# First mixer of a two-layer trunk: nineteen block transfers a group on another queue, and a third place between dependent steps of the triangular solve

## The chip, the cores and the metric

The kernel runs on one core of a Trainium2 chip. The core has a matrix engine (TensorE, PE in the profile, its weight loads PEld), a vector engine (VectorE, DVE), an activation engine (ScalarE, ACT), a general engine (GpSimd, POOL) and a synchronising engine (SyncE, SP). Each engine works through its own instructions in order. Transfers between HBM and on-chip memory are issued by SyncE or by GpSimd, each on a queue of its own. The metric is the device time of one execution in microseconds, lower is better.

## The reference

A decoder trunk of two layers works on one sequence of 256 positions with 2048 features, all in float32. Layer 0 mixes with gated DeltaNet, layer 1 with sparse attention; behind each mixer stand a residual layer norm, a gated convolutional feed-forward part and a small gated update. The change lies in the mixer of layer 0, whose core is this (cut):

```python
kb = k * beta[..., None]
vb = v * beta[..., None]
diff = gc[..., :, None] - gc[..., None, :]
decay = jnp.where(tri, jnp.exp(jnp.where(tri, diff, 0.0)), 0.0)
lmat = jnp.where(strict, jnp.einsum('bhncd,bhnsd->bhncs', kb, k) * decay, 0.0)
amat = lmat + jnp.eye(C, dtype=jnp.float32)
rhs = jnp.concatenate([vb, kb * jnp.exp(gc)[..., None]], axis=-1)
sol = lax.linalg.triangular_solve(amat, rhs, left_side=True, lower=True, unit_diagonal=True)
qk = jnp.where(tri, jnp.einsum('bhncd,bhnsd->bhncs', q, k) * decay, 0.0)
...
def step(S, inp):
    v_new = u_n - jnp.einsum('bhck,bhkv->bhcv', w_n, S)
    o_n = jnp.einsum('bhck,bhkv->bhcv', qd_n, S) + jnp.einsum('bhcs,bhsv->bhcv', qk_n, v_new)
    S = S * gl_n[..., None, None] + jnp.einsum('bhck,bhcv->bhkv', kd_n, v_new)
```

Here q, k and v are projections of the input with a short causal convolution, beta and the decays gc come from two small gates, and each of 32 value heads has a unit lower triangular system to solve. The output of each head is normed and gated with a projection z, and a last projection joins the heads.

## The kernel before

**Tiling.** Every large product streams its float32 weights from HBM in pieces of 512 KB (`raw`, four buffers). ScalarE copies each piece into the form that TensorE multiplies (`hi`, line 127), VectorE takes the rest (`lo`, line 128), and TensorE multiplies both; `hi` and `lo` have three buffers each. SyncE's queue carries these pieces, and a piece can be asked for when the `lo` of the piece four before it is written.

**Groups.** The first mixer treats the 32 value heads in eight groups of four. A group's sequence is cut into two halves of 128 positions (index `a`), and each half into four blocks of 32 (index `b`). The order of the weight products is: `values(g)`, then `keys(g + 1)` with the queries, then `zgate(g + 1)`, then the next group. Behind `values(7)` and in place of further keys the output projection is begun (`ahead`).

**Places.** The small work of a group is written as generators that yield. The weight products call `next(self.inter)` after every few matmuls; each call is a place, and the generator runs on to its next yield there. `behind` ties an instruction behind the weight matmul issued last, as order alone, without a semaphore; `late` does the same for all groups but the first, whose front work is emitted at once inside `values(0)`. A planner then orders each engine's instructions by its own estimate of when each is ready, by the order of emission and by raised priorities (the splits of weights, the copies and hops of the solve). An instruction tied to a place can come later than it, not earlier. `pause(n)` leaves n places empty, and `flush` runs what is left of a generator at once.

- `front(g + 1)` runs in the 27 places of `zgate(g + 1)`: `fetch` (the gates' rows, `qd`), `decays` and `sums`, `blocks` (the matrix `L` and its diagonal blocks to `lt` in HBM), `causal` (the masked decays `dm`, in tile `qd`; line 530 clips, line 532 takes the exponential; then the gram `gt`, whose blocks go to `lo` in HBM), and for all groups but the first `pieces` (`ld` read back from `lt`).
- `substitute` inverts the 32 x 32 diagonal blocks on GpSimd out of `ld`, one row after another (lines 685 and 687), and sends them to `tt` in HBM.
- `inverses` loads them into `pm`, and the off-diagonal blocks from `lo` into `LB`. It is called behind `keys(g + 1)`, once the places of the solve before are used up.
- `solve` runs in the places of the next `values` and `keys`, 24 each (42 in all for group 6, where part of the output projection takes the keys' place): per block a product with the inverse (`y_ps`, line 773), ScalarE's copy of it (`ys`, line 776), and for the next block a product with the earlier solutions (`l_ps`, line 766) and VectorE's step to the new right side (`ts`, line 769), called a hop here. Three hops stand in each half.
- `outputs` follows in the same places: two sets of products (`o_ps`), their squares, an inverse root, VectorE's gating (line 806) into `ot`. The transposes of `ot` (line 812) are handed on to the next `zgate` or `ahead`.

In `finish`, the solve and the outputs of one group take 38 yields before the change; group 0 has four more empty places ahead. The mixes of the next group run beside them from the ninth place.

Weights and the transfers of `qd`, `rd`, `lt`, `lo`, `ld`, `rr` and `LB` share SyncE's queue; `tt`, `pm` and the constants are on GpSimd's, which also computes `substitute` in the same order of instructions.

Of the kernel before, what the change touches and what calls it, by code (L numbers as in the profile page):

```python
# [12 lines left out]
AF = mybir.ActivationFunctionType  # L13
# [46 lines left out]
def bcast(ap, n, axis):  # L60

    dims = [list(x) for x in ap.ap]
    dims.insert(axis, [0, n])
    return bass.AP(tensor=ap.tensor, offset=ap.offset, ap=dims)


class Trunk:
# [393 lines left out]
    def gdn_groups(self, pool, gk, cw, ng, oT, load, gates, ahead):  # L461
# [4 lines left out]
        nc, t = self.nc, self.t  # L466
# [3 lines left out]
        LB = pool.tile([P, 2, 6, P], F32, tag="LB", name="LB")  # L470
# [6 lines left out]
        pause = lambda n: itertools.repeat(None, n)  # L477
# [19 lines left out]
        def late(s, ins):  # L497
            return self.behind(ins) if s["g"] else ins
# [19 lines left out]
        def causal(s):  # L518

            g, dm = s["g"], s["qd"]  # L520
            do = s["qo"] = pool.tile([P, 4, P], F32, tag="qo", name="qo", bufs=2)
            for h in h4:
                late(s, nc.scalar.activation(do[:, h], dm[:, 1, h], AF.Exp, bias=self.gout[:, 4 * g + h:4 * g + h + 1]))
            yield
            n21 = s["n21"] = pool.tile([P, 4, P], F32, tag="n21", name="n21", bufs=2)
            nc.vector.tensor_tensor(five(n21), bcast(s["gram"][0][:, :, P:S], 2, 2), five(do), op=ALU.mult)
            for a in range(2):
                for h in h4:
                    gc = self.gc[:, a, 4 * g + h:4 * g + h + 1]
                    late(s, nc.vector.scalar_tensor_tensor(dm[:, a, h], dm[:, a, h], gc, self.qmin,  # L530
                                                           op0=ALU.subtract, op1=ALU.min))
                nc.scalar.activation(dm[:, a], dm[:, a], AF.Exp)
                yield
            gt = s["gt"] = pool.tile([P, 2, 4, P], F32, tag="ld" if g else "L", name="gt")
            for a, ps in enumerate(s["gram"]):
                nc.vector.tensor_tensor(five(gt[:, a]), bcast(ps[:, :, 0:P], 2, 2), five(dm[:, a]), op=ALU.mult)
            yield
            sq = s["sq"] = pool.tile([P, 2, S], F32, tag="y0", name="sq")
            nc.scalar.activation(sq, s["q"], AF.Square)
            xm = s["xm"] = pool.tile([P, 4, 16], F32, tag="xm", name="xm")  # L540
            nc.vector.tensor_tensor(xm, bcast(s["x8"].rearrange("p q e -> p (q e)"), 4, 1), bcast(self.blk, 16, 2),
                                    op=ALU.mult)
            yield from pause(2)
            lo = s["lo"] = self.dr.tile([32, 2, 4, 6, 32], F32, tag="lb", name="lo")
            for c in range(3):
                late(s, nc.sync.dma_start(
                    out=lo.rearrange("k a h n j -> k (a h) (n j)")[:, :, 32 * pair(c, c + 1):][:, :, :96 - 32 * c],
                    in_=gt[32 * c:32 * c + 32, :, :, 32 * c + 32:].rearrange("k a h i -> k (a h) i")))
                yield
            if g:  # L550
                yield
                pieces(s)
# [69 lines left out]
        def blocks(s):  # L622

            g, c, L = (s[x] for x in ("g", "c", "L"))
            for a, ps in enumerate(s["gram"]):
                for h in h4:
                    nc.vector.scalar_tensor_tensor(L[:, h, a], ps[:, h // 2, 0:P], c[:, a, h // 2, h % 2:h % 2 + 1],
                                                   L[:, h, a], op0=ALU.mult, op1=ALU.mult)
                yield
            yield  # L630
            lt = s["lt"] = self.dr.tile([8, 4, 32, 32], F32, tag="lt", name="lt")
            for b in range(4):
                late(s, nc.sync.dma_start(
                    out=lt[:, b].rearrange("q i j -> i q j"),
                    in_=L[32 * b:32 * b + 32, :, :, 32 * b:32 * b + 32].rearrange("p h a j -> p (h a) j")))
            yield

        def pieces(s):

            ld = s["ld"] = pool.tile([P, 32, 32], F32, tag="ld", name="ld")  # L640
            for e in h4:
                late(s, nc.sync.dma_start(out=ld[32 * e:32 * e + 32], in_=bass.AP(
                    tensor=s["lt"].tensor, offset=s["lt"].offset, ap=[[1024, 32], [1, 1024]])))

        def mixes(s):
# [46 lines left out]
        def inverses(s):  # L692

            for h in h4:
                nc.gpsimd.dma_start(out=pm[32 * h:32 * h + 32, :, :, 32 * h:32 * h + 32].rearrange("p a b j -> p (a b) j"),
                                    in_=s["tt"][2 * h:2 * h + 2].rearrange("a b c e j -> (c e) (a b) j"))
            for h in h4:
                for a in range(2):
                    self.behind(nc.sync.dma_start(out=LB[32 * h:32 * h + 32, a, :, 32 * h:32 * h + 32],
                                                  in_=s["lo"][:, a, h]))  # L700

        def values(s):
            g = s["g"]
# [41 lines left out]
        def solve(s):  # L745
            u = s["u"] = pool.tile([P, 2, 4, P], F32, tag="u", name="u")
            bank = lambda name: self.sp.tile([P, P], F32, tag="bk", name=name)
            for a in range(2):
                if a:
                    ps = self.sp.tile([P, 4, 4, 32], F32, tag="bk", name="x_ps")  # L750
                    for h in h4:
                        self.behind(nc.tensor.matmul(ps[:, :, h], u[:, 0, h],
                                                     s["n21"][:, h].rearrange("p (b i) -> p b i", b=4),
                                                     start=True, stop=True))
                    with self.tc.high_priority():
                        nc.vector.scalar_tensor_tensor(s["v1"], ps, -2.0, s["v1"], op0=ALU.mult, op1=ALU.add)
                    yield from pause(2)
                    s["turn"](1)
                    yield from pause(2)
                y = pool.tile([P, 4, P], F32, tag="y", name="ys", bufs=2)  # L760
                for b in range(4):
                    r = s["vs"][:, b]
                    if b:
                        ps = bank("l_ps")
                        for c in range(b):
                            self.behind(nc.tensor.matmul(ps, LB[:, a, pair(c, b)], y[:, c], start=not c, stop=c == b - 1))
                        r = pool.tile([P, P], F32, tag="ts", name="ts")
                        with self.tc.high_priority():
                            nc.vector.scalar_tensor_tensor(r, ps, s["s8"][:, b, 1, a:a + 1], s["vs"][:, b],
                                                           op0=ALU.mult, op1=ALU.add)  # L770
                        yield from pause(2)
                    ps = bank("y_ps")
                    self.behind(nc.tensor.matmul(ps, pm[:, a, b], r, start=True, stop=True))
                    with self.tc.high_priority():
                        if b < 3:
                            nc.scalar.activation(y[:, b], ps, AF.Copy)
                        for h in h4:
                            nc.scalar.activation(u[32 * b:32 * b + 32, a, h], ps[32 * h:32 * h + 32], AF.Copy)
                    yield from pause(2)
                yield  # L780

        def outputs(s):
# [41 lines left out]
        def finish(s, n):  # L824

            steps = [itertools.chain(pause(0 if s["g"] else 4), solve(s), outputs(s))]
            if n is not None:
                steps.append(itertools.chain(pause(8), mixes(n)))
            while steps:
                yield  # L830
                steps = [x for x in steps if next(x, steps) is not steps]

        def front(s):
            return itertools.chain(fetch(s), decays(s), sums(s), blocks(s), causal(s))
# [5 lines left out]
        rest, s = [], keys(0)  # L840
        for g in range(8):
# [18 lines left out]
            if g < 7:  # L860
                substitute(n)
                self.inter = finish(s, n)
                s = n
# [441 lines left out]
```

## Time and profile before

| | us |
|---|---|
| median of 3 runs (2774.4, 2787.5, 2786.63) | 2786.63 |
| the profiled execution | 2776.45 |
| its span | 2773.4 |
| TensorE busy in the span | 2739.2 |
| VectorE, ScalarE, GpSimd busy | 1860.1, 1487.1, 354.3 |

The profiled execution takes 3 us more than its span, which runs from its first to its last instruction. The first mixer's groups fill about the first 765 us; each group takes some 85.

A row of order of time reads: start in us from the span's start, length in us, engine, line, operation, what it writes and from what, shapes, how many were merged into the row; in square brackets the idle time of the engine before it and what ended it. SPq is SyncE's queue. A row of waits reads: who waited, for whom, microseconds in total, number of times, the longest. A row of stretches holds the stretch and its length, then busy time and number of instructions for PE, PEld, DVE, ACT and POOL, the granted TensorE clock as a share of full speed, the DMA engines' share and GB/s. A row of groups ends with total busy us and mean ns of one, then the idle time before them and what ended it.

### The profile page before, as it was taken

What the parts mean: (1) busy time and instruction counts of PE and PEld (TensorE: products, weight loads), DVE (VectorE), ACT (ScalarE), POOL (GpSimd) and SP (SyncE); (2) the same over time, 40 slices, a digit from 0 to 9 for tenths busy, and PEclk for the clock granted to TensorE, in tenths of its full rate; (3) what the DMA queues carried; (4) which work ended last, traced back from release to release, by engine and by line L of the source; (5) the groups of instructions that cost most, each with busy time, mean ns of one, the idle gap of its engine ahead of it and who ended that gap; (6) DMA issues with size and microseconds to landing.
All of it is one profiled execution on the core that took longest, in us unless ns stands there. A gap on an engine that the chain in (4) does not pass through costs nothing. (4 is left out here: it accounts for less than half of the span.)

```text
span 2773.4 us, 40001 instructions
## 1 busy us (share of the span) xinstructions
PE 2739.2 (99%) x14604; PEld 2356.4 (85%) x14604; DVE 1860.1 (67%) x3109; ACT 1487.1 (54%) x2512; POOL 354.3 (13%) x682
## 2 busy tenths in 40 slices
PE   9999999999999999999999999999999999999999
PEld 7888888888888888888888889888888888888887
DVE  7878787877556666666545766775676666655566
ACT  5666666666545555555434544455455555543444
POOL 1554333554000000000000000210000000000000
PEclk9999999999999999999999999999999999999999
DMA  7766767666575666766666567545566666656655
GB/s 224 195 188 169 183 171 181 153 176 175 167 240 162 188 209 203 209 199 203 193 195 206 182 184 232 175 144 165 175 190 197 196 191 194 199 192 191 211 171 193
DMA packets 435140, 525.08 MB, mean 189 GB/s; under 512 B 50976, under 2 KB 324496, under 8 KB 434688
## 3 DMA queue, kind: packets, MB, share of 16 engines
q1 hardware_dynamic: 427952, 504.05, 60.9%
q0 software_dynamic: 6992, 18.49, 2.7%
q8 instruction: 114, 1.87, 0.3%
q14 instruction: 82, 0.67, 0.1%
HBM read 516.62 MB, written 8.97 MB: 190 GB/s over the span
## 5 line engine op out<-in xcount | busy, mean ns | idle before, releaser
L128 DVE TENSOR_TENSOR lo<-raw,hi 128x1024 fp32r<-128x1024 f32 (+1 forms) x920 | 1123.3, 1223 | 600.8 <-ACT hi L127 584.2
L127 ACT ACTIVATE hi<-raw 128x1024 fp32r<-128x1024 f32 (+1 forms) x920 | 966.8, 1053 | 656.4 <-PE mm_ps L202 400.3
L160 PE MATMUL mm_ps<-xT,hi 128*128 128x512 f32 (+1 forms) x4176 | 1036.3, 396 | 6.8 <-DVE xT L242 5.7
L160 PEld LDWEIGHTS mm_ps<-xT,hi 128*128 128x128 f32 (+1 forms) x4176 | 764.8, 189 | 153.8 <-ACT hi L241 5.6
L164 PE MATMUL mm_ps<-xT,lo 128*128 128x256 f32 (+1 forms) x4176 | 557.9, 284 | 0.9 <-DVE lo L128 0.9
L164 PEld LDWEIGHTS mm_ps<-xT,lo 128*128 128x128 f32 (+1 forms) x4176 | 538.3, 191 | 22.1 <-DVE lo L128 1.7
L199 PE MATMUL mm_ps<-hi,xT 128*128 128x512 f32 (+1 forms) x704 | 272.6, 388 | 0.0
L202 PE MATMUL mm_ps<-hi,xT 128*128 128x512 f32 (+1 forms) x704 | 268.8, 383 | 0.0
L237 ACT ACTIVATE fold<-mm_ps 128x256 f32<-128x256 f32 x261 | 98.3, 377 | 266.2 <-PE mm_ps L160 266.0
L199 PE MATMUL mm_ps<-hi,hTA 128*128 128x512 f32 x512 | 199.2, 389 | 0.0
L202 PE MATMUL mm_ps<-hi,hTA 128*128 128x512 f32 x512 | 199.2, 389 | 0.0
L206 PE MATMUL mm_ps<-lo,xT 128*128 128x512 f32 (+1 forms) x704 | 187.8, 383 | 0.0
L256 POOL DMA_DIRECT2D lng<-in_ln_g x16 | 8.8, 551 | 1239.1 <-PE mm_ps L206 661.1
L685 POOL TENSOR_TENSOR xt<-ld,xi 128x60 f32<-128x60 f32 (+24 forms) x248 | 124.4, 501 | 305.3 <-DMA ld<-lt 286.5
L202 PEld LDWEIGHTS mm_ps<-hi,xT 128*128 128x128 f32 x704 | 132.2, 188 | 24.2
L199 PEld LDWEIGHTS mm_ps<-hi,xT 128*128 128x128 f32 x704 | 132.1, 188 | 23.7
L206 PEld LDWEIGHTS mm_ps<-lo,xT 128*128 128x128 f32 x704 | 130.1, 188 | 24.9
L206 PE MATMUL mm_ps<-lo,hTA 128*128 128x512 f32 x512 | 136.8, 389 | 0.0
L687 POOL TENSOR_TENSOR xi<-xi,xt 128x60 f32<-128x60 f32 (+24 forms) x248 | 119.2, 481 | 19.4
L202 PEld LDWEIGHTS mm_ps<-hi,hTA 128*128 128x128 f32 x512 | 96.1, 188 | 20.0
L206 PEld LDWEIGHTS mm_ps<-lo,hTA 128*128 128x128 f32 x512 | 96.1, 188 | 20.0
L199 PEld LDWEIGHTS mm_ps<-hi,hTA 128*128 128x128 f32 x512 | 96.1, 188 | 19.9
(264 smaller groups left out, 2570.4 us busy)
## 6 DMA issues: line engine op xcount, KB each, us to landing
raw<-in_gdn_w_in SPq DMA_DIRECT2D x192, 512.0 KB, 4.8
raw<-in_ffn_w_gate SPq DMA_DIRECT2D x160, 512.0 KB, 4.0
raw<-in_ffn_w_up SPq DMA_DIRECT2D x160, 512.0 KB, 4.1
raw<-in_ffn_w_down SPq DMA_DIRECT2D x160, 512.0 KB, 4.1
raw<-in_dsa_w_in SPq DMA_DIRECT2D x72, 512.0 KB, 3.7
raw<-in_gdn_w_o SPq DMA_DIRECT2D x64, 512.0 KB, 4.0
raw<-in_ple_w_gate SPq DMA_DIRECT2D x64, 512.0 KB, 4.9
raw<-in_dsa_w_o SPq DMA_DIRECT2D x32, 512.0 KB, 3.8
```

Source lines behind the costliest of these rows:

```text
L127: act = nc.scalar.activation(hi, raw, AF.Copy)
L128: ins = nc.vector.tensor_tensor(lo, raw, hi.bitcast(F32), op=ALU.subtract)
L160: ins = nc.tensor.matmul(q[:m, :], hi[:, k, o:o + m], x[:, k0 + k].rearrange("p a b -> p (a b)"), start=k0 + k == 0, stop=last)
L164: ins = nc.tensor.matmul(q[:m, S:], lo[:, k, o:o + m], x[:, k0 + k, 0, :], start=False, stop=last)
L199: ins = nc.tensor.matmul(ps[a][:, :n], xh, hi, start=k == 0, stop=False)
L202: self.before = self.recent = nc.tensor.matmul(ps[a][:, :n], xl, hi, start=False, stop=False)
L206: self.last = self.recent = nc.tensor.matmul(ps[a][:, :n], x(k)[:, 0, a * P:(a + 1) * P], lo, start=False, stop=k == kt - 1)
L237: nc.scalar.activation(t[:m], ps[:, S:], AF.Copy)
L256: ins = self.nc.gpsimd.dma_start(out=r, in_=bass.AP(tensor=src.tensor, offset=src.offset, ap=[[0, P], [1, n]]))
L685: nc.gpsimd.tensor_tensor(tmp[:, :m, :w], bcast(ld[:, i + 1:, i], m, 1), xi[:, :m, i:i + 1].to_broadcast([P, m, w]), op=ALU.mult)
L687: nc.gpsimd.tensor_tensor(xi[:, :m, i + 1:], xi[:, :m, i + 1:], tmp[:, :m, :w], op=ALU.subtract)
```

## The change

Three edits, all in the first mixer:

1. The transfers of `L`'s diagonal blocks to HBM (`lt`, four a group), of the gram's blocks (`lo`, three), the reading back (`ld`, four) and the loading of the off-diagonal blocks (`LB`, eight) are issued by GpSimd in place of SyncE. `LB`'s are no longer tied behind the last weight matmul; the others stay tied as before.
2. Behind each hop of VectorE in the solve, and behind the first product of the first half (`y_ps` of `a` = 0, `b` = 0, which ScalarE copies), three places instead of two.
3. In `causal` each exponential over `dm` is issued one place after the four clips before it and is tied to that place; the gram's products follow one place after the second.

```diff
@@ causal
                     late(s, nc.vector.scalar_tensor_tensor(dm[:, a, h], dm[:, a, h], gc, self.qmin,
                                                            op0=ALU.subtract, op1=ALU.min))
-                nc.scalar.activation(dm[:, a], dm[:, a], AF.Exp)
                 yield
+                late(s, nc.scalar.activation(dm[:, a], dm[:, a], AF.Exp))
+            yield
@@ causal
             for c in range(3):
-                late(s, nc.sync.dma_start(
+                late(s, nc.gpsimd.dma_start(
                     out=lo.rearrange("k a h n j -> k (a h) (n j)")[:, :, 32 * pair(c, c + 1):][:, :, :96 - 32 * c],
@@ blocks
             for b in range(4):
-                late(s, nc.sync.dma_start(
+                late(s, nc.gpsimd.dma_start(
                     out=lt[:, b].rearrange("q i j -> i q j"),
@@ pieces
             for e in h4:
-                late(s, nc.sync.dma_start(out=ld[32 * e:32 * e + 32], in_=bass.AP(
+                late(s, nc.gpsimd.dma_start(out=ld[32 * e:32 * e + 32], in_=bass.AP(
@@ inverses
             for h in h4:
                 for a in range(2):
-                    self.behind(nc.sync.dma_start(out=LB[32 * h:32 * h + 32, a, :, 32 * h:32 * h + 32],
-                                                  in_=s["lo"][:, a, h]))
+                    nc.gpsimd.dma_start(out=LB[32 * h:32 * h + 32, a, :, 32 * h:32 * h + 32], in_=s["lo"][:, a, h])
@@ solve
                             nc.vector.scalar_tensor_tensor(r, ps, s["s8"][:, b, 1, a:a + 1], s["vs"][:, b],
                                                            op0=ALU.mult, op1=ALU.add)
-                        yield from pause(2)
+                        yield from pause(3)
@@ solve
-                    yield from pause(2)
+                    yield from pause(2 if a or b else 3)
```

## The prediction

> **What bounds the kernel now.** I read the page's busy shares first, then the waits of the matmul engine, then order of time around its longest waits.
>
> ```profile
> PE 2739.2 (99%) x14604; PEld 2356.4 (85%) x14604; DVE 1860.1 (67%) x3109; ACT 1487.1 (54%) x2512; POOL 354.3 (13%) x682
> ```
> ```profile
> PE l_ps L766 <- ACT ys L776: 13.0, 6, 2.9
> ...
> PE y_ps L773 <- DMA pm<-tt: 2.9, 1, 2.9
> ...
> PE y_ps L773 <- ACT hi L127: 1.4, 5, 0.3
> ```
>
> TensorE is busy for 2739.2 of 2773.4 us, so no edit to queues and places can bring more than the 34 us in which it is not, and these rows hold 17.3 of them, all in the first mixer's solve. The large one comes once in each of six groups: l_ps, the first product after the first block's solution, waits for ScalarE's first copy. One group in order of time, first TensorE, then ScalarE, then SyncE's queue:
>
> ```profile
> 468.89 1.98 PE L160 MATMUL mm_ps<-xT,hi 128*128 128x512 f32 x8
> 470.71 0.38 PE L773 MATMUL y_ps<-vs,pm 128*128 128x128 f32 x2
> 470.85 2.15 PE L164 MATMUL mm_ps<-xT,lo 128*128 128x256 f32 x16
> 474.86 0.49 PE L766 MATMUL l_ps<-ys,LB 128*128 128x128 f32 x2 [1.85 <-ACT ys L776]
> 475.10 3.51 PE L160 MATMUL mm_ps<-xT,hi 128*128 128x512 f32 x8
> ```
> ```profile
> 468.50 0.63 ACT L532 ACTIVATE qd<-qd 128x512 f32<-128x512 f32 x1 [1.97 <-DVE qd L530]
> 469.03 0.58 ACT L738 ACTIVATE zs<-mm_ps 128x512 f32<-128x512 f32 x1
> 471.63 1.06 ACT L127 ACTIVATE hi<-raw 128x1024 fp32r<-128x1024 f32 x1 [2.01 <-DMA raw<-in_gdn_w_in]
> 472.60 0.61 ACT L532 ACTIVATE qd<-qd 128x512 f32<-128x512 f32 x1
> 473.11 0.58 ACT L738 ACTIVATE zs<-mm_ps 128x512 f32<-128x512 f32 x1
> 473.59 1.04 ACT L127 ACTIVATE hi<-raw 128x1024 fp32r<-128x1024 f32 x1
> 474.54 0.27 ACT L776 ACTIVATE ys<-y_ps 128x128 f32<-128x128 f32 x1
> ```
> ```profile
> 459.43 0.37 SPq L620 DMA_DIRECT2D rd<-rs  x1
> 461.93 3.22 SPq L122 DMA_DIRECT2D raw<-in_gdn_w_in  x2
> 465.25 4.72 SPq L633 DMA_DIRECT2D lt<-L  x4
> 470.06 4.28 SPq L122 DMA_DIRECT2D raw<-in_gdn_w_in  x3
> ```
>
> The copy stands seventh in ScalarE's order. The first exponential holds ScalarE for 1.97 us until VectorE has written its operand; then a split waits 2.01 us for weights; then a second exponential, a tanh and a split stand before the copy. On SyncE's queue the four transfers of L take 4.72 us, and no weight is asked for between 465 and 470.
>
> The eight matmuls from 468.89 to 470.71 are two places of the order, so **a place is 0.91 us**. And a stall is dearer than its idle time: the eight matmuls after it last 3.51 us instead of 1.98. The stretches around the stalls show why; the first and the last of four such rows (the other two are at 471 and at 557):
>
> ```profile
> 386.00:394.00 8.00, 5.07 (x25) 4.29 (x24) 5.89 (x11) 4.12 (x9) 0.00 (x0) 0.79 1.07 311
> ...
> 642.00:650.00 8.00, 6.07 (x26) 4.92 (x25) 4.93 (x7) 5.60 (x14) 0.00 (x0) 0.79 1.00 287
> ```
>
> The column behind POOL is the granted clock: 0.79. By the matmul rows one such drop costs 3.51 - 2.10 = 1.4 us (2.10 as in the row below), four of them 5.6. Two of the six stalls have none; one of them:
>
> ```profile
> 223.97 0.49 PE L766 MATMUL l_ps<-ys,LB 128*128 128x128 f32 x2 [1.78 <-ACT ys L776]
> 224.22 2.10 PE L160 MATMUL mm_ps<-xT,hi 128*128 128x512 f32 x8
> ```
>
> So a gap of 1.78 us kept the clock, and one of 1.85 lost it. [...]
>
> **The change, part by part.**
>
> *A third place behind the first copy.* It puts 0.91 us of weight matmuls between y_ps and l_ps in every group that stalls: 6 x 0.91 = 5.5 us off the 13.0. The copy does not get later by it, as it depends on y_ps alone. It is covered by matmuls that have to run anyway; at the end of the group the cover is thinner, see below.
>
> *Exponentials a place later.* Between the landing of the weights and the copy stands one exponential, 0.51 us from its start to the next. If it goes behind the copy, that is 6 x 0.5 = 3.0; if the planner leaves it, because VectorE and not its place decides when it is ready, nothing. The wait of 1.97 before it is followed by the wait for weights, and so not worth its length by itself. I take half, 1.5.
>
> *Transfers on GpSimd's queue.* SyncE loses 19 issues a group: four of L, three of the gram, four of ld, eight of LB. The next rows show what the eight hold up: they stand before the fetch of the gates' rows, and ScalarE and, behind it, VectorE wait for these.
>
> ```profile
> 276.23 5.04 SPq L699 DMA_DIRECT2D LB<-lo  x8
> 281.37 0.39 SPq L503 DMA_DIRECT2D qd<-grow  x1
> ```
> ```profile
> ACT L L513 <- DMA qd<-grow: 16.4, 6, 3.6
> ```
> ```profile
> L128 DVE TENSOR_TENSOR lo<-raw,hi 128x1024 fp32r<-128x1024 f32 x8 | 9.8, 1219 | 2.5 <-ACT hi L127 2.5
> ```
>
> The fetch can be issued up to 5.0 us earlier, which removes most of 16.4 / 6 = 2.7 us of ScalarE's waiting a group and the 2.5 us that VectorE stands idle in this one. How much reaches the copy is not to be read: the late weights were asked for at 461.93, before L's transfers, so taking those away does not bring them sooner; they land late behind rd, which stays. Only if the whole stretch runs earlier do they. Bounds: nothing, and all that the first two parts leave, 13.0 - 5.5 - 1.5 = 6.0. I take 2.5, somewhat under half, because the weights' own issue is not moved.
>
> [...]
>
> What it costs on GpSimd:
>
> ```profile
> L695 POOL DMA_DIRECT2D pm<-tt x32 | 18.6, 591 | 12.5 <-DMA tt<-xi 12.0
> ```
> ```profile
> L685 POOL TENSOR_TENSOR xt<-ld,xi 128x60 f32<-128x60 f32 (+24 forms) x248 | 124.4, 501 | 305.3 <-DMA ld<-lt 286.5
> ```
> ```profile
> 276.08 2.33 POOL L695 DMA_DIRECT2D pm<-tt  x4
> ```
> ```profile
> 302.70 0.38 PE L773 MATMUL y_ps<-vs,pm 128*128 128x128 f32 x2
> ```
>
> 19 x 0.59 = 11.2 us a group, into 286.5 / 8 = 35.8 us in which GpSimd waits for ld. If LB's eight go ahead of pm, pm's last issue ends 4.7 us later, at 283 instead of 278.4, and the next group's first y_ps needs it at 302.7. In the first group, where pm is late already (the 2.9), the same order falls into GpSimd's wait for tt; there I see between -2.9 and +2 and take 0. Behind pm's wait for tt on GpSimd then stand L's transfers; a substitution that starts some us later still ends within those 20.
>
> *A third place behind each of VectorE's hops.* The five waits of y_ps put down to a split, 1.4 us, are each at most 0.3, under a place. That they are for ts is my reading: the split named is not an operand of y_ps. All of it: -1.4.
>
> *What seven places more push back.* A solve has three hops in each half: six places, and one for the first copy. The gates and the transposes behind them come 7 x 0.91 = 6.4 us later; in the last two groups about 4 x 0.91 = 3.6, because there the steps that find no place are emitted at once. The margins of these two, the group before the last first:
>
> ```profile
> 697.80 0.86 DVE L806 SCALAR_TENSOR_TENSOR ot<-o_ps,rs,zs 128x128 f32<-128x128 f32 x3
> ```
> ```profile
> 701.39 0.60 PE L812 MATMUL ot_ps<-ident,ot 128*128 128x128 f32 x4
> ```
> ```profile
> 747.59 0.16 DVE L797 SCALAR_TENSOR_TENSOR of<-oss,wq 128x4 f32<-128x4 f32 x1 [0.20 <-ACT sqs L796]
> ```
> ```profile
> 753.23 1.12 DVE L806 SCALAR_TENSOR_TENSOR ot<-o_ps,rs,zs 128x128 f32<-128x128 f32 x4
> ```
> ```profile
> 759.60 1.03 PE L812 MATMUL ot_ps<-ident,ot 128*128 128x128 f32 x8
> ```
>
> In the first of them all gates are done at 698.7, 2.7 us before the first transposes, which need only the first half's, four of 0.28 us earlier; in the second they are done at 754.4, 5.2 us before. A shift of 3.6 us uses up the one and leaves 1.6 of the other: between 0 and +1.5, I take +0.5.
>
> **Sum.** First copies -5.5 - 1.5 - 2.5 = -9.5, of 13.0, which leaves 3.5. Clock: at 3.5 us in six places one drop stays at most, 3 x 1.4 = -4.2. Hops -1.4. Tail +0.5. Together **-14.6 us**, 2776.45 to 2761.9 for the profiled execution. That one is 10.2 us below the median of the runs; of the four executions known, two are at 2774.4 and 2776.45, two at 2786.63 and 2787.5, and nothing in the trace says why. I set the base at their mean, 2781.2, which gives 2766.6, rounded **2767**.
>
> **Rivals.** *Only the places count.* The weights land when they did, and the exponential stays before the copy. For: the late weights were issued before L's transfers. Against: the 2.7 us of ScalarE's waiting for the fetch. -5.5; gaps of 2.0 remain in the two groups that had over 2.8, with their clock drops, so -2.8; hops -1.4, tail +0.5: -9.2, 2772.0.
>
> *The copy slides along.* Put later, both exponentials stand straight before the copy: 2 x 0.5 against one now, 0.5 later, and GpSimd's transfers compete with weights at this point; together they take the place's 0.91. For: the order of ScalarE shows how near the exponentials stand. Then only the hops gain, 2779.8.
>
> *Slower: VectorE's backlog.* The gates and the inverse roots ahead of them go from the end of the keys into the z stretch, before the causal work. In the last group they take from 747.59 to 754.35, 6.8 us, less the two splits of 1.22 that run in between: 4.3 us of VectorE. If they push its queue in every group, exponentials and copy are later by as much: 6 x (4.3 - 0.9) = +20.4, two more clock drops +2.8, hops -1.4: +21.8, 2803. It decides from the point where more than 0.91 us gets through to the copy. Against: the 2.5 us idle of VectorE that an earlier fetch gives back, and that the copy itself needs nothing from VectorE.
>
> **How the numbers follow.** Forecast 0.55, places only 0.25, sliding copy 0.12, backlog 0.08. Within 0.5% (14 us, about what a measurement here can tell from no change) of 2786.63 means 2772.7 to 2800.6. Of the forecast 0.44 lies under 2772.7, of the places' case, which ends right at it, 0.11: faster 0.55. The backlog beyond 2800.6 gives slower 0.07, the rest 0.38. Low end: all of 13.0 + 5.6 + 1.4 + 2.9 = 22.9 off the profiled 2776.45, 2753. High end: the sliding copy from the two upper executions, 2787.
>
> **What would show it.** l_ps's wait for ys falls from 13.0 to 3.5 or less, y_ps's for ts goes; the granted clock around the first copies is 1.0 in at least three of the four stretches. SyncE's queue has no transfers of L between weights, and the fetch is issued 4 to 5 us earlier against the first z matmul. If ScalarE's wait for weights before the copy keeps its 2 us, the transfers gave nothing. The prediction is wrong if l_ps keeps more than 8 us of waits, or if TensorE waits for ot, pm or LB.

## The result, and the profile after

The changed kernel takes **2768.7 us** (median of 17 executions, 2763.33 to 2776.38) against 2783.74 (17 executions, 2774.4 to 2787.5): ratio 0.9948, 95% interval 0.9940 to 0.9957. The profiled execution after took 2766.34 us, its span 2763.9 us, 9.5 less than the span before.

First, the waits of TensorE after the change (who waited for whom, total us, times, longest):

```profile
PE y_ps L773 <- DMA pm<-tt: 7.8, 1, 7.8
...
PE v_ps L725 <- DVE v L756: 2.2, 3, 1.4
PE l_ps L766 <- ACT ys L776: 2.1, 6, 0.5
```

The 13.0 us of l_ps are gone. The 2.1 that bear the same name belong to another product, the second l_ps of block 2. The waits of y_ps for a split (1.4) and for ts (0.5) are gone too. New are 7.8 us for pm, once, in the first group, and 2.2 us for the right sides.

One group in order of time: TensorE, then ScalarE.

```profile
471.16 0.38 PE L773 MATMUL y_ps<-vs,pm 128*128 128x128 f32 x2
471.30 2.15 PE L164 MATMUL mm_ps<-xT,lo 128*128 128x256 f32 x16
473.29 1.09 PE L160 MATMUL mm_ps<-xT,hi 128*128 128x512 f32 x4
474.22 0.38 PE L766 MATMUL l_ps<-ys,LB 128*128 128x128 f32 x2
```
```profile
461.77 0.63 ACT L533 ACTIVATE qd<-qd 128x512 f32<-128x512 f32 x1 [0.21 <-DVE qd L530]
...
464.25 0.63 ACT L533 ACTIVATE qd<-qd 128x512 f32<-128x512 f32 x1
...
471.36 1.06 ACT L127 ACTIVATE hi<-raw 128x1024 fp32r<-128x1024 f32 x1 [0.68 <-PE mm_ps L160]
472.32 0.26 ACT L776 ACTIVATE ys<-y_ps 128x128 f32<-128x128 f32 x1
```

The third place is there (four more matmuls at 473.29), and l_ps starts without idle time. But ScalarE's order has changed far more than by a place: both exponentials run seven and more us ahead of the copy, and not between the split and the copy. VectorE's order says why; its gates and its clips in the same group, before and then after (the z matmuls of this group begin at 444.4 and at 444.8):

```profile
443.75 1.38 DVE L806 SCALAR_TENSOR_TENSOR ot<-o_ps,rs,zs 128x128 f32<-128x128 f32 x5
...
459.91 0.86 DVE L627 SCALAR_TENSOR_TENSOR L<-g_ps,c,L 128x128 f32<-128x128 f32 x3
...
467.32 1.14 DVE L530 SCALAR_TENSOR_TENSOR qd<-qd,gc,cst 128x128 f32<-128x128 f32 x4
```
```profile
449.55 1.38 DVE L806 SCALAR_TENSOR_TENSOR ot<-o_ps,rs,zs 128x128 f32<-128x128 f32 x5
460.32 0.35 DVE L530 SCALAR_TENSOR_TENSOR qd<-qd,gc,cst 128x128 f32<-128x128 f32 x1
...
466.44 0.87 DVE L628 SCALAR_TENSOR_TENSOR L<-g_ps,c,L 128x128 f32<-128x128 f32 x3
```

The gates ended 0.8 us behind the first z matmul and now end 6.1 us behind it, 5.4 us later, where seven places are 6.4. The planner turned the rest round: the clips, which stood behind L's products, now stand ahead of them.

ScalarE's waits in the stretch from 138 to 670 us, after; before, the fetch of the gates' rows cost 16.4, the clips 13.7 and the weights 13.9 in the same stretch:

```profile
ACT hi L127 <- DMA raw<-in_gdn_w_in: 10.5, 7, 2.1
...
ACT qd L533 <- DVE qd L530: 3.3, 6, 2.2
ACT L L513 <- DMA qd<-grow: 1.3, 1, 1.3
```

The first group, GpSimd first (the first of LB's eight transfers, tt, pm), then TensorE, then one stretch with its clock:

```profile
97.76 0.62 POOL L700 DMA_DIRECT2D LB<-lo  x1
...
129.39 2.33 POOL L691 DMA_DIRECT2D tt<-xi  x4 [0.31 <-POOL xi L688]
141.35 2.33 POOL L696 DMA_DIRECT2D pm<-tt  x4 [9.63 <-DMA tt<-xi]
```
```profile
147.39 0.77 PE L773 MATMUL y_ps<-vs,pm 128*128 128x128 f32 x2 [7.83 <-DMA pm<-tt]
147.81 3.31 PE L160 MATMUL mm_ps<-xT,hi 128*128 128x512 f32 x8
```
```profile
146.00:154.00 8.00, 6.61 (x37) 5.99 (x38) 1.49 (x2) 2.30 (x6) 5.11 (x10) 0.72 0.62 184
```

LB's eight transfers, from 97.76 to 106.6 us, fell into the middle of the substitution, tt was sent 6.4 us later than before (122.96), and the clock dropped behind the stall. That is the only drop left in the solves; the four behind first copies are gone. LB accounts for less than half of the 6.4 us: the substitution took 39.0 us instead of 36.1, and the other 3.6 us are its later start, at 90.40 instead of 86.83, when ld had landed.

By the profiles the span's 9.5 us are made up so: l_ps -10.9, clock -5.6 + 1.2 (eight matmuls in 3.31 instead of 2.10), y_ps behind VectorE and ScalarE -1.9, pm +4.9, v_ps +2.2: -10.1. The medians differ by more, 15.0: the profiled execution before the change lay 7.3 us below its median, that after it 2.4, and what the rows leave out isn't known. Part of it may be l_ps: in x3_exps and x5_rd_late below, which take as long as the kernel before and were profiled at 2781.16 and 2784.79 us, it waits 17.0 and 16.6 us and not 13.0.

### The profile page after: what moved, and what is told of

It is laid out like the page before. It is cut to its first block, busy times and chain, and to the rows that moved or that the text cites. A ratio compares the mean times of both kernels' runs of the same rounds, so it can differ in the third digit from the quotient of the medians.

```text
span 2763.9 us, 40071 instructions
## 1 busy us (share of the span) xinstructions
PE 2734.6 (99%) x14604; PEld 2352.4 (85%) x14604; DVE 1854.1 (67%) x3109; ACT 1489.0 (54%) x2512; POOL 437.4 (16%) x834
## 5 line engine op out<-in xcount | busy, mean ns | idle before, releaser
L686 POOL TENSOR_TENSOR xt<-ld,xi 128x60 f32<-128x60 f32 (+24 forms) x248 | 117.6, 474 | 27.9 <-DMA ld<-lt 9.5
```

The costliest lines, as they stand in the source:

```text
L686: nc.gpsimd.tensor_tensor(tmp[:, :m, :w], bcast(ld[:, i + 1:, i], m, 1), xi[:, :m, i:i + 1].to_broadcast([P, m, w]), op=ALU.mult)
```

## The experiments

Each ran beside the kernel before on the same chip, and the ratios are against that (its medians there: 2780.05 to 2781.7).

| kernel | what it is | median us | ratio | 95% |
|---|---|---|---|---|
| x1_places | third places alone | 2759.69 | 0.9924 | 0.9912 to 0.9936 |
| x2_queue | transfers alone | 2790.25 | 1.0033 | 1.0021 to 1.0045 |
| x3_exps | exponentials alone | 2781.79 | 1.0002 | 0.9994 to 1.0011 |
| x4_places_exps | after, transfers on SyncE | 2759.36 | 0.9924 | 0.9912 to 0.9936 |
| x7_gates_late | before, outputs 7 places later | 2766.78 | 0.9952 | 0.9936 to 0.9968 |
| x6_rd_rows | before, rd as rows, early | 2782.58 | 1.0003 | 0.9994 to 1.0013 |
| x10_rows_late | before, rd as rows, late | 2765.80 | 0.9951 | 0.9937 to 0.9964 |
| x12_elements_late | before, rd in elements, late | 2784.76 | 1.0007 | 0.9998 to 1.0016 |
| x9_all_rows | x4 with rd as rows, late | 2751.94 | 0.9900 | 0.9886 to 0.9913 |
| x11_after_rows | after with rd as rows, late | 2756.77 | 0.9918 | 0.9905 to 0.9932 |
| x8_group0_sync | after, first group's transfers on SyncE | 2764.05 | 0.9947 | 0.9930 to 0.9963 |
| x5_rd_late | before, rd's line moved | 2780.60 | 1.0000 | 0.9990 to 1.0009 |

### Which of the three edits brings the time

**The third places alone.**

```diff
-                        yield from pause(2)
+                        yield from pause(3)
-                    yield from pause(2)
+                    yield from pause(2 if a or b else 3)
```

> The kernel before with the third places alone, transfers and exponentials as they were. Theory A (the transfers' queue brings the first copy forward, the places only cover what is left): l_ps keeps 13.0 - 5.5 = about 7.5 us of waits for the copy, two of the four clock drops stay, y_ps's 1.4 us go; 9 us under before, about 2774.5, and the first group's wait for pm stays near 2.9. Theory B (the places alone do it all): no wait of l_ps over 0.5 us, 15 us or more under before. Theory C (the copy slides along with the places): l_ps keeps over 11 us, 0 to 2 us under before.

**The transfers alone**, in all of `lt`, `lo`, `ld`, `LB`:

```diff
-                late(s, nc.sync.dma_start(
+                late(s, nc.gpsimd.dma_start(
```

> The kernel before with the nineteen transfers on GpSimd's queue alone, two places and early exponentials as before. Theory A: the fetch of the gates' rows is issued 4 us or more earlier, ScalarE's wait for it falls from 16.4 to under 3 us, the first copy comes in time even for two places, l_ps waits for it under 3 us, no clock drop around it; y_ps keeps its 1.4 us; the first group's pm comes late, 5 us or more more waiting than the 2.9; net 9 to 13 us under before. Theory B: l_ps keeps 10 us or more, at most 3 us under before, or slower by the first group's 5 us.

**The exponentials alone.**

```diff
-                nc.scalar.activation(dm[:, a], dm[:, a], AF.Exp)
                 yield
+                late(s, nc.scalar.activation(dm[:, a], dm[:, a], AF.Exp))
```

> The kernel before with the exponentials and the gram's products a place later, alone. By the prediction's term 0 to 3 us under before: one exponential of 0.5 us leaves the way of the copy or does not. If VectorE's queue and not the place decides when the exponentials run, their order on ScalarE is as before, and l_ps keeps 12 to 14 us.

**Places and exponentials**, the changed kernel with its transfers back on SyncE:

```diff
-                late(s, nc.gpsimd.dma_start(
+                late(s, nc.sync.dma_start(
```

> The changed kernel with all transfers back on SyncE's queue (places and exponentials kept). Theory A: like the places alone, l_ps keeps 4.5 to 7.5 us, 9 to 12 us under before; the first group's wait for pm is back near 2.9, which the changed kernel has at 7.8. Theory B: as fast as the changed kernel or faster by those 5 us, 15 to 20 us under before.

TensorE's waits, of x1_places, of x2_queue, of x4_places_exps:

```profile
PE l_ps L766 <- ACT ys L776: 6.5, 6, 2.3
```
```profile
PE l_ps L765 <- ACT ys L775: 17.4, 6, 3.8
PE y_ps L772 <- DMA pm<-tt: 7.1, 1, 7.1
```
```profile
PE l_ps L767 <- ACT ys L777: 2.0, 3, 1.4
```

The places alone bring 21 us (0.76% of 2781), twice what the prediction gave them with their clock and hops (9.7). The exponentials bring nothing, alone or with the places. The transfers cost: 9 us alone (interval 5.8 to 12.5), and 0.9948 / 0.9924 puts the changed kernel some 7 us above x4_places_exps. The gain was forecast from the wrong edits. Of the expectations for x1_places none fits whole: its time is that of theory B, its 6.5 us at l_ps are near theory A. These 6.5 come from the slowest of its six executions (2766.64), and all but 0.8 of them are waits for the second copy of a group, not the first.

### Why places bring so much

x7_gates_late leaves the solve's places as they were before (two behind each hop and behind the first copy) and puts seven empty ones behind the solve, so the gates, and they alone, come as late as after the change.

```diff
-itertools.chain(pause(0 if s["g"] else 4), solve(s), outputs(s))
+itertools.chain(pause(0 if s["g"] else 4), solve(s), pause(7), outputs(s))
```

> The kernel before with seven empty places between the solve and its outputs and no third place anywhere in the solve. Theory D: the planner issues rd at 19 us or later behind the first z matmul instead of 15, and the first exponential at about 20 instead of 25; l_ps waits under 5 us though it has two places alone, y_ps keeps its 1.4 to 2 us; 12 to 18 us under before. Theory P: l_ps keeps 12 us or more, no gain.

```profile
PE l_ps L766 <- ACT ys L776: 4.5, 6, 1.6
```

13.4 us are won without a single matmul more between y_ps and l_ps. The waits of y_ps behind the hops, put down to a split (1.4), stay, as they must, for these lack their third place. So most of the places' gain is the later gates and the order of instructions that the planner makes behind them. One group of this run, whose z matmuls begin at 439.9; SyncE's queue, then ScalarE:

```profile
459.35 0.37 SPq L620 DMA_DIRECT2D rd<-rs  x1
```
```profile
467.42 0.26 ACT L776 ACTIVATE ys<-y_ps 128x128 f32<-128x128 f32 x1
...
471.69 1.06 ACT L127 ACTIVATE hi<-raw 128x1024 fp32r<-128x1024 f32 x1 [2.50 <-DMA raw<-in_gdn_w_in]
```

rd is issued 19.5 us behind the first z matmul, where before the change it was 15.1 (459.43 against 444.4), and the first exponential runs at 19.4 us in place of 24.1; theory D expected both, and 12 to 18 us. ScalarE's wait for late weights hasn't gone by this: from 138 to 670 us it is 20.1 us in place of 13.9. But in each of the six groups that stall in the kernel before it stands ahead of the first copy, and here in five of them behind it; the sixth has none. There it costs less, as 4.5 us at l_ps say. The remaining 8 us between this run and x1_places are left for the cover itself and the hops; they weren't taken apart further.

### What made the first copy late

The prediction saw weights land late behind rd and left it at that. rd is a row of 256 numbers, written to HBM element by element, 1 KB. The issues of the stretch of the kernel before around it, from 459 to 465 us (KB each, median us to landing):

```profile
raw<-in_gdn_w_in SPq DMA_DIRECT2D x2, 512.0 KB, 8.9
rd<-rs SPq DMA_DIRECT2D x1, 1.0 KB, 8.0
```

and the DMA engines meanwhile (the last three columns are clock, DMA share, GB/s):

```profile
464.50:467.50 3.00, 3.00 (x15) 2.49 (x14) 3.00 (x6) 1.60 (x2) 0.00 (x0) 1.00 0.56 50
```

50 GB/s, where the page has a mean of 189. Four runs take rd apart.

**rd's line moved**, behind L's transfers in the program:

```diff
-            late(s, nc.sync.dma_start(out=rd.rearrange("j p -> p j"), in_=rk.rearrange("p (j a) -> p a j", a=2)[:, 1]))
 ...
+            late(s, nc.sync.dma_start(out=rd.rearrange("j p -> p j"), in_=s["rk"].rearrange("p (j a) -> p a j", a=2)[:, 1]))
```

> The kernel before with one edit: the transfer rd (256 elements of 4 bytes to HBM) is issued behind the transfers of L instead of some 10 us earlier. Theory D (the weights piece that the splits ahead of the first copy wait for lands late because rd's small elements hold up the transfers behind it; the gates moved back made the planner issue rd later, past that piece): that piece lands in 4 to 6 us instead of 9, ScalarE's 2 us of waiting for it go, l_ps waits under 5 us instead of 13, 8 to 16 us under before. Theory P (the third places cover the late copy, rd has no part): l_ps keeps 12 us or more, no change of over 2 us.

The planner issued it ahead of L's transfers all the same, 15 to 17 us behind the first z matmul as before. The time is that of before, and the run tells nothing.

**rd as two rows of 512 B**: TensorE transposes the column, ScalarE copies it, one transfer writes two rows.

```diff
+            pr = self.sp.tile([2, P], F32, tag="bk", name="r_ps")
+            late(s, nc.tensor.transpose(pr, s["rk"].rearrange("p (j a) -> p a j", a=2)[:, 1], self.ident))
+            yield
+            rs = pool.tile([P, P], F32, tag="sqs", name="rrow")[0:2]
+            nc.scalar.activation(rs, pr, AF.Copy)
+            rd = s["rd"] = self.dr.tile([2, P], F32, tag="rd", name="rd")
+            late(s, nc.sync.dma_start(out=rd, in_=rs))
```

> The kernel before with rd turned by TensorE and written as two rows of 512 bytes in place of 256 elements of 4 bytes, at the place of the run with rd issued late. Theory D: no weights piece lands later than 7 us in the z stretches, rd itself lands in under 5 us instead of 8, the first group's wait for pm (2.9) goes, l_ps waits under 5 us; 10 to 18 us under before, and at least as fast as rd merely issued late. Theory P: as with rd issued late, no change; or slower by a few us for the added transposes and copies. If weights still land after 8 to 10 us, not the small elements hold them up.

```profile
PE r_ps L636 <- DVE rs L287: 18.0, 7, 3.5
```

The waits for weights, for the first copy and for pm were all gone, and the time was the same: the transposition stood in TensorE's order ahead of VectorE's root and waited 18.0 us for it. The cost had only changed places.

**The same rows, the transposition at the end of `causal`**, when the root is long done:

```diff
                     in_=gt[32 * c:32 * c + 32, :, :, 32 * c + 32:].rearrange("k a h i -> k (a h) i")))
                 yield
+            pr = self.sp.tile([2, P], F32, tag="bk", name="r_ps")
+            late(s, nc.tensor.transpose(pr, s["rk"].rearrange("p (j a) -> p a j", a=2)[:, 1], self.ident))
+            rs = pool.tile([P, P], F32, tag="sqs", name="rrow")[0:2]
+            nc.scalar.activation(rs, pr, AF.Copy)
+            rd = s["rd"] = self.dr.tile([2, P], F32, tag="rd", name="rd")
+            late(s, nc.sync.dma_start(out=rd, in_=rs))
```

> The kernel before with one thing changed: the row rd is turned by TensorE and written as two rows of 512 B, as in x6_rd_rows, but the transposition stands at the end of the steps of causal, some seven places later, where VectorE's root has long ended. Theory D' (the 256 four-byte elements of rd hold the weights behind them up, these hold the first copy up, and in x6_rd_rows the gain went into the 18.0 us for which the transposition waited for the root): l_ps waits under 4 us instead of 13.0, r_ps waits under 2 us, pm under 3, weights behind rd landing within 5 us, and the time 2766 to 2772, 10 to 15 under before. Rival (VectorE's queue, with the gates ahead of the clips, is what ends the first copy's wait, and rd only shows beside it): l_ps keeps 10 or more and the time is 2778 to 2784.

TensorE's waits, then ScalarE around the first copy:

```profile
PE l_ps L771 <- ACT ys L781: 4.8, 5, 1.8
```
```profile
464.93 0.63 ACT L532 ACTIVATE qd<-qd 128x512 f32<-128x512 f32 x1 [2.51 <-DVE qd L530]
...
466.10 1.04 ACT L127 ACTIVATE hi<-raw 128x1024 fp32r<-128x1024 f32 x1
467.11 0.63 ACT L532 ACTIVATE qd<-qd 128x512 f32<-128x512 f32 x1
...
468.13 1.05 ACT L127 ACTIVATE hi<-raw 128x1024 fp32r<-128x1024 f32 x1
469.07 0.27 ACT L781 ACTIVATE ys<-y_ps 128x128 f32<-128x128 f32 x1
```

This is the order ahead of the copy that the prediction quoted, with one thing out of it: the 2.01 us for weights. ScalarE still waits for the clips (2.51). l_ps fell from 13.0 to 4.8 and no stretch of 8 us in the solves has a granted clock under 0.96; the gain is 13.6 us by the ratio. The rows give as much: l_ps -8.2, the four drops -5.6, pm -2.9, and y_ps's waits for ts +2.8 (3.3 instead of 0.5). l_ps was expected under 4; the time, 2765.80, lies just under the 2766 to 2772 expected. As much is won here as in x7_gates_late, with clips and exponentials as late as before. So taking the late weights out of the way of the first copy is enough for such a gain, and the turned order of clips and L's products isn't needed for it; whether it adds anything in x7_gates_late wasn't separated.

**The place alone.** In x10_rows_late rd is written at another place as well as in another form. Here it is written late in the order, in elements:

```diff
                     in_=gt[32 * c:32 * c + 32, :, :, 32 * c + 32:].rearrange("k a h i -> k (a h) i")))
                 yield
+            rd = s["rd"] = self.dr.tile([2, P], F32, tag="rd", name="rd")
+            late(s, nc.sync.dma_start(out=rd.rearrange("j p -> p j"), in_=s["rk"].rearrange("p (j a) -> p a j", a=2)[:, 1]))
```

> x10_rows_late changed two things about rd, its form (two rows of 512 B for 256 elements of 4 B) and its place in the order of SyncE's queue (behind L's four transfers for ahead of two fetches of weights and these transfers). This run changes the place alone: the kernel before with rd's four-byte write at the end of causal's steps, no transposition. If the form is what costs, the slow stretch is still there, only behind later weights: ScalarE's waits for raw stay at 10 us or more over groups 1 to 6, L's transfers ahead of it land faster, the first copy's wait becomes smaller but does not go (3 to 10 us), pm's wait stays at 2 or more, and the time is 2770 to 2778. If the place is what cost, the waits for raw go and the time is that of x10_rows_late, 2764 to 2768.

The issues around rd (472 to 479 us), then ScalarE's wait for weights over groups 1 to 6:

```profile
raw<-in_gdn_w_in SPq DMA_DIRECT2D x3, 512.0 KB, 11.3
...
rd<-rs SPq DMA_DIRECT2D x1, 1.0 KB, 9.7
```
```profile
ACT hi L127 <- DMA raw<-in_gdn_w_in: 33.1, 9, 5.7
```

The slow landings moved with rd, ScalarE waits 33.1 us for weights instead of 13.9, and l_ps waits 14.7: 3.9 for first copies, the rest for second ones, as the late weights now come behind the first. The form is what costs, not the place: a ratio of 1.0007 here, 0.9951 with rows at the same place (x10_rows_late). Only the first group's wait for pm, expected at 2 or more, went. The time was expected at 2770 to 2778 and did not fall at all; that the elements would hurt as much at the later place was not foreseen.

The groups' medians to landing from 150 to 680 us show the same on L's transfers, before and in x10_rows_late:

```profile
lt<-L SPq DMA_DIRECT2D x24, 32.0 KB, 7.1
```
```profile
lt<-L SPq DMA_DIRECT2D x24, 32.0 KB, 2.9
```

### What rd costs the changed kernel, and what the queue costs

**x4_places_exps with rd as rows**, by the edit of x10_rows_late:

> x4_places_exps (2759.4) with rd written as rows by the late transposition of x10_rows_late. Theory D': the places have already taken the first copy out of the way of late weights, so little is left: l_ps 2.0 to under 1, about 3 us of transposition and copies added and the 1 to 2 us of waits for raw gone: 2756 to 2761. Rival (rd still costs in x4 through the weights behind the first copy, whose splits wait for raw): 2750 to 2755.

**The changed kernel with rd as rows**, by the same edit:

> The kernel after (transfers on GpSimd's queue) with rd written as rows in the same way. If the 9 us which the transfers cost against x4_places_exps come from rd's slow stretch falling on them and on the first group's transposed blocks, it comes near x9_all_rows: pm under 3 us and 2757 to 2762. If they come from the queue itself (the issues of 0.59 us on GpSimd's engine inside its substitution, ld and tt landing later), pm stays at 6 to 8 us and the time is 2764 to 2769.

From TensorE's waits in the two:

```profile
PE l_ps L772 <- ACT ys L782: 0.2, 1, 0.2
```
```profile
PE v_ps L730 <- DVE v L761: 3.0, 4, 1.4
```

**x9_all_rows, 2751.94 us, is the fastest kernel of the case**, 28 us under before and, by the ratios, 13 under the changed kernel. Its l_ps waits come to 0.2, and from 138 to 670 us ScalarE waits for no weights. It came faster than the 2756 to 2761 of the theory under test: its rival, that rd still costs through the weights behind the first copy, was right.

In x11_after_rows the wait for pm is gone, though LB's transfers are still on GpSimd; its 2756.77 us lie just under the 2757 to 2762 expected. In the changed kernel tt is sent (129.39) behind rd (126.85), in the kernel before ahead of it (122.96 and 124.95). The issues from 120 to 132 us, after and in x11_after_rows:

```profile
raw<-in_gdn_w_in SPq DMA_DIRECT2D x4, 512.0 KB, 8.3
tt<-xi POOLq DMA_DIRECT2D x4, 32.0 KB, 9.4
rd<-rs SPq DMA_DIRECT2D x1, 1.0 KB, 9.6
```
```profile
raw<-in_gdn_w_in SPq DMA_DIRECT2D x4, 512.0 KB, 4.1
tt<-xi POOLq DMA_DIRECT2D x4, 32.0 KB, 2.5
```

With rd out of the way the transfers on GpSimd still cost 0.9918 / 0.9900, about 5 us of the 7. Of these, v_ps holds 3.0; the rest isn't settled.

**The first group's transfers back on SyncE**, the rest as after:

```diff
-                late(s, nc.gpsimd.dma_start(
+                late(s, (nc.gpsimd if g else nc.sync).dma_start(
```

> The changed kernel with the first group's nineteen transfers back on SyncE's queue, the other groups' on GpSimd's. If GpSimd's issuing inside the first substitution is what makes pm late, TensorE's wait for it falls from 7.8 to 3 us or less, the half clock behind it goes, and the time falls by 5 to 8 us against the changed kernel, to 20 to 22 us under before, as fast as the places alone. If it is the slow stretch behind rd that holds tt, the wait keeps over 6 us.

```profile
PE l_ps L769 <- ACT ys L779: 5.0, 5, 1.7
PE y_ps L776 <- DMA pm<-tt: 3.0, 1, 3.0
```

tt is sent at 122.96 again, ahead of rd (125.32), and pm's wait fell from 7.8 to 3.0; l_ps rose from 2.1 to 5.0. So what the changed kernel added to the 2.9 of before took both, the transfers on GpSimd, by which tt came behind rd, and rd's elements. By the first z matmul of each group it is 4.8 us ahead of after at the third group (194.2 against 199.0) and level at the seventh (525.9 against 525.8). Its ratio is that of the changed kernel: what the first group gave was lost again in the next ones, and the 5 to 8 us expected didn't come.

## Why the prediction was right, and where it was not

The time was right: 2767 forecast, 2768.7 measured, and l_ps, the hops and the clock went as the sum said. But two of its terms were off by about 10 us each, one either way, and cancelled each other: that the total fits is luck.

*First copies, -9.5 of 13.0.* l_ps lost 10.9, the mechanism only in part. The step "it puts 0.91 us of weight matmuls between y_ps and l_ps" is true (473.29 above) and small. The step that failed is "What seven places more push back", costed at +0.5 for the last two groups' transposes: the gates' move into the z stretch, which the rival of VectorE's backlog took for a loss, was the main gain (x7_gates_late, 13.4 us with no place added in the solve). The planner issued rd later behind it, and ScalarE's wait for late weights fell behind the first copy, where it had stood ahead of it; that this wait ahead of the copy is worth as much shows in x10_rows_late. The rival had found the place, and had its sign wrong: it let VectorE's queue shift as it stood, where the planner orders it anew. With clock and hops the places were given 9.7 (5.5, 2.8 and 1.4) and brought 21.

*Exponentials, -1.5.* Nothing: x3_exps is at a ratio of 1.0002, and x4_places_exps has the time of x1_places.

*Transfers, -2.5.* This term had the wrong sign, +7 to +9 in its place. The failed step is "I take 2.5, somewhat under half": the fetch did come earlier (ScalarE waits 1.3 us for it and not 16.4; with the transfers alone, 11.1), but nothing of that reached the copy, for which l_ps waits 17.4 us in x2_queue. The prediction had the reason in hand, "they land late behind rd, which stays", and gave it no price. L's transfers did not land sooner from the other queue: from 150 to 680 us it took 8.2 us by the median from GpSimd's queue in the changed kernel, and 8.1 from SyncE's in x4_places_exps.

*First group, 0 between -2.9 and +2.* It was +4.9 and a clock drop of 1.2, outside the bounds. The step "the same order falls into GpSimd's wait for tt" failed: LB's eight were put into the substitution instead, which also began 3.6 us later, and tt then met rd. The same step's claim for later groups holds; no wait for pm or LB came there.

*Clock, -4.2.* All four drops went (-5.6) and the first group's came (+1.2): -4.4. *Hops, -1.4*: as forecast. *Tail, +0.5*: no wait for ot at all. The sum had no term for v_ps, +2.2. This wait is in the changed kernel, x8_group0_sync and x11_after_rows, and not in x1_places, x4_places_exps or x9_all_rows; its cause wasn't followed up.

*The base.* The prediction read two pairs into four executions and took their mean, 2781.2. Seventeen executions lie from 2774.4 to 2787.5 with a median of 2783.74; the profiled one was near the low end.

*The rivals.* Only the places count (2772.0) named the right edit and undersized it: x1_places took 2759.69. The sliding copy did not come; nor did the backlog.

## What to carry to other kernels

Where several edits are forecast together, run each alone: here one brought 21 us, one cost 7 to 9 and one did nothing, and the sum looked like the forecast. When a transfer lands late, look at what was issued shortly before it on any queue, and count that transfer's elements as well as its bytes: here 1 KB in 256 elements took 8.0 us to land, and weights of 512 KB around it 8.9, where around the same 1 KB in two rows they landed in 3.8 (x10_rows_late, 465 to 472 us). Where a planner writes the order, moving one group of instructions back changes the order of all that come behind; read the new order of each engine before pricing it as a shift.

## What was not expected of the hardware

- 1 KB written to HBM as 256 elements of 4 B took 8.0 us to land in the kernel before (459 to 465 us) and 9.6 after the change (120 to 132 us), and transfers issued around it landed late: weights of 512 KB in 8.9 us in the kernel before, 11.3 in x12_elements_late and 8.3 after the change, where x11_after_rows has 4.1 in the same stretch, and the 32 KB blocks of tt in 9.4 after the change, where x11_after_rows has 2.5. Written as two rows behind a transposition, rd left ScalarE no wait for weights from 138 to 670 us (x10_rows_late; 13.9 in the kernel before). Over eight groups it was worth 13.6 us in the kernel before, 8 in the changed one and 7 in x4_places_exps (by the ratios of the table). Why other transfers land late beside the elements, no run shows.
- In x4_places_exps TensorE stood for 1.41 us, and then ran at half clock (0.50 from 312 to 316 us), where the kernel before kept its clock behind 1.78 (the row at 223.97 in the prediction):

```profile
309.86 0.49 PE L767 MATMUL l_ps<-ys,LB 128*128 128x128 f32 x2 [1.41 <-ACT ys L777]
```
```profile
312.00:314.00 2.00, 2.00 (x6) 1.52 (x6) 0.43 (x3) 0.00 (x0) 0.00 (x0) 0.50 0.71 244
```

  In the first group of the kernel before, eight matmuls behind a gap of 2.89 us (the wait for pm that ends at 142.21) took 2.10 us, and the granted clock was 1.00 from 138 to 146, so the clock held there too. In these rows it was lost behind 1.41 and 1.85 us (the row at 474.86 in the prediction) and held behind 1.78 and 2.89: the length of the gap alone does not tell them apart, and what does isn't settled here. The 1.41 us are followed by 1.21 us of eight matmuls of one column; no run shows whether these have a part in it.
